# A hybrid decoder block on Trainium2: the norms of queries and keys, one tile of tokens at a time or four

## The chip, the cores and the metric

The kernel runs on one core of a Trainium2 chip. The metric is the device time of one execution in microseconds; lower is better. The engines are named as in the profile: PE (TensorE; PEld is its weight load), DVE (VectorE), ACT (ScalarE), POOL (GpSimd) and SP (SyncE, which here only issues DMAs).

## The reference

One decoder block over 1024 tokens of width 1024. Two token mixers run side by side: an attention of 8 heads of width 64 with a forgetting term, and a diagonal state-space model (SSM). Their gated sum goes through a projection, and a mixture of 32 experts follows. What matters here is the start of the attention:

```python
q = _rmsnorm(q.reshape(b, s, N_HEADS_ATTN, HEAD_DIM), q_norm_g[l])
k = _rmsnorm(k.reshape(b, s, N_HEADS_ATTN, HEAD_DIM), k_norm_g[l])
...
logits = jnp.einsum('bhqd,bhkd->bhqk', qb, kf) + cb[..., :, None] - cum[:, :, None, :]
```

where `_rmsnorm(x, g)` is `x * rsqrt(mean(x*x) + 1e-6) * g`, over the 64 values of one head. So for every token and head there is one factor for the query and one for the key.

## The kernel before

Tokens lie in tiles of 128 along the partitions, eight tiles in all. A matrix in 32-bit float is split into a high part and a remainder, so a product is three matmuls. The kernel goes through the SSM, the gates, the attention, the output projection with the router, and the experts, in this order; parts of neighbouring stages run into each other.

The attention takes two heads at a time, four pairs, and a pair in two halves of four tiles (512 tokens). Three generators do the work, and `run_all` interleaves their steps by a key, so that matmuls of one fill PE while others wait:

- `proj` (lines 783 to 813) computes queries, keys and values of one half. For each of its four tiles, 24 matmuls of 384 columns (lines 795 to 797) go into one PSUM bank; ACT copies queries and keys to the tile `qk` (800) and squares them in PSUM (801); DVE sums each group of 64 squares into four columns of `ss` (802) and takes the remainder of the values (807). Then comes the norm: scale and epsilon on DVE (808), a power with exponent -1/2 on POOL into `rstd` (809), and the multiplication of the 256 columns by the four factors, on POOL in place (811). `ss` and `rstd` have room for four tiles of tokens, four columns each. It is called eight times: for pair 0 half 0, pair 0 half 1, pair 1 half 0, and so on.
- `prep` (815 to 869) transposes the scaled keys (821) and queries (824) of a half, four tiles each, on PE; ACT and DVE split them into `KX`, `KY`, `QX`, `QY` (833 to 839); PE computes scores (852, with a mask at 855) only to find each row's maximum, by a reduction on DVE (857, 860). The maxima are transposed (862) and stored into rows of `QX` by two DMAs from POOL's queue (868, 869). Its transposes come some steps after the `proj` that it needs: in the meantime the next `proj` and an `attend` have put their own steps on PE.
- `attend` (871 to 941) computes scores again (901 to 904), takes the exponential twice on ACT (907, 909), forms the remainder `pL` on DVE (910), adds up the row sums on POOL (912, over `pe`, which has three buffers), and multiplies by the values (886, 887). At its end DVE splits the sums (`sh` on ACT, 923; `sl` on DVE, 925), PE spreads them (930) and DVE takes reciprocals (933) and scales.

During the last pair, `mixed_ssm` (its matmuls are at lines 700 to 702) fills PE, and line 671 splits its inputs on DVE.

The order within an engine's queue isn't the program's alone. A planner takes the instructions in program order as a priority, simulates when each could start, and gives an engine the first one that it believes ready. It also sets all semaphores. An engine then works through its queue in that order: an instruction whose input is late holds up all that stand behind it on that engine.

Of the kernel before, what the change touches and what calls it, by code (L numbers as in the profile page):

```python
# [16 lines left out]
ALU = mybir.AluOpType  # L17
AX = mybir.AxisListType

P = 128  # L20
# [5 lines left out]
DH = 64  # L26
G = 32
CG = 16
EPS = 1e-6
# [13 lines left out]
def hybrid_block(ctx: ExitStack, tc: tile.TileContext, t, out):  # L43

    nc = tc.nc
# [14 lines left out]
    def mmtile():  # L60
        return psA.tile([P, 512], F32, tag="A", name="psA_t")
# [4 lines left out]
    def f32(ap):  # L66
        return ap.bitcast(F32)
# [4 lines left out]
    def slot(name, shape=(S,), dt=F32, where=None):  # L72
        pl, n = where or (slab, SLOTS)
        return pl.tile([P] + list(shape), dt, tag="s4", name=name, bufs=n)
# [60 lines left out]
    mhalf = cp.tile([P, 4], F32, name="mhalf")  # L135
# [352 lines left out]
    with ExitStack() as st:  # L488
# [19 lines left out]
        for b in range(G // GB):  # L508
# [84 lines left out]
            for q4 in range(GB // 4):  # L593
# [7 lines left out]
                for r in range(4):  # L601
                    g = q4 * 4 + r
                    o = ps[:, r * P:(r + 1) * P]
# [179 lines left out]
    def proj(p_, half):  # L783

        qk = slot("qk", (4, 256))
        ss = ap_.tile([P, 4, 4], F32, name="ss", bufs=2)
        rstd = ap_.tile([P, 4, 4], F32, name="rstd", bufs=2)
        for r in range(4):
            i = half * 4 + r
            ps = mmtile()  # L790
            for k in range(KD):
                ah = hTh[k][:, i * P:(i + 1) * P]
                al = hTl[k][:, i * P:(i + 1) * P]
                wh, wl = p_.w[k]
                nc.tensor.matmul(ps[:, :384], ah, wh, start=(k == 0), stop=False)  # L795
                nc.tensor.matmul(ps[:, :384], ah, wl, start=False, stop=False)  # L796
                nc.tensor.matmul(ps[:, :384], al, wh, start=False, stop=(k == KD - 1))  # L797
                if k in (2, 5):
                    yield
            nc.scalar.copy(qk[:, r, :], ps[:, 0:256])  # L800
            nc.scalar.activation(ps[:, 0:256], ps[:, 0:256], AF.Square)
            nc.vector.tensor_reduce(ss[:, r, :], ps[:, 0:256].rearrange("p (a b) -> p a b", b=64),
                                    axis=AX.X, op=ALU.add)
            vs = ps[:, 256:384].rearrange("p (a b) -> p a b", b=64)
            vh = p_.V[:, i, :, 0, :]
            nc.scalar.copy(vh, vs)
            nc.vector.tensor_tensor(p_.V[:, i, :, 1, :], vs, f32(vh), ALU.subtract)
            nc.vector.tensor_scalar(ss[:, r, :], ss[:, r, :], 1.0 / DH, EPS, op0=ALU.mult, op1=ALU.add)
            nc.gpsimd.tensor_tensor(rstd[:, r, :], ss[:, r, :], mhalf, ALU.pow)
            q3 = qk[:, r, :].rearrange("p (a b) -> p a b", b=64)  # L810
            nc.gpsimd.tensor_tensor(q3, q3, rstd[:, r, :].unsqueeze(2).to_broadcast([P, 4, 64]), ALU.mult)
            yield
        p_.qk = qk

# [127 lines left out]

    cur = new_pair(0)
    run_all((proj(cur, 0), 12, 0, 1))
    run_all((proj(cur, 1), 12, 0, 1), (prep(cur, 0), 10, 0.3, 1))
    for pr in range(4):
        if pr < 3:
            nxt = new_pair(pr + 1)
            run_all((attend(cur, 0), 10, 0.1, 1), (proj(nxt, 0), 12, 0, 1), (prep(cur, 1), 10, 0.25, 1))
            if pr < 2:  # L950
                run_all((attend(cur, 1), 18, 0.1, 1), (proj(nxt, 1), 12, 0, 1), (prep(nxt, 0), 10, 0.3, 1))
            else:
                fill = mixed_ssm()
                run_all((attend(cur, 1), 18, 0.1, 1), (proj(nxt, 1), 12, 0, 0.9), (prep(nxt, 0), 10, 0.3, 1),
                        (itertools.islice(fill, 5), 5, 0.9, 1.1))
            cur = nxt
        else:
            wq_stack.close()
            slab2 = pool(ctx, "slab2")
            S2 = (slab2, SLOTS2)  # L960
            y3 = []
            ya, wgs = [], []

            def ready_a():

                for k in range(3):
                    ya.append(split_slot("a", yaT_d[k * P:(k + 1) * P, :], where=S2))
                    yield
                for mg in (0, 2):
                    wgs.append(mixed_weights(0, mg))  # L970
                    yield

            run_all((attend(cur, 0), 10, 0, 1), (itertools.islice(fill, 16), 16, 0, 1),
                    (prep(cur, 1), 10, 0.25, 1))
            run_all((attend(cur, 1, y3), 18, 0.1, 1), (fill, 32, 0, 1), (ready_a(), 5, 0.5, 0.95))
# [542 lines left out]
```

## Time and profile before

| | us |
|---|---|
| median of 3 runs | 1182.69 (1181.40 to 1185.41) |
| profiled execution | 1180.84 |
| its span | 1179.2 |
| PE busy | 1106.0 (94%) |
| DVE busy | 804.9 (68%) |
| ACT busy | 620.3 (53%) |
| POOL busy | 356.9 (30%) |

The mean granted clock of PE is 0.98. Line 808 has 32 instructions on DVE, line 809 has 32 and line 811 has 32 on POOL. They lie between 327.2 and 568.1 us of the span.

How to read the profile: the page's slices are 40 equal parts of the span, each digit the busy tenths of an engine. A row of the view by groups gives line, engine, operation, output<-input with shapes, count, then busy us, mean ns of one, and the idle time of the engine just before these instructions with what ended it. A row of the timeline gives start and duration in us, then the same names, and in brackets the idle time before it. A row of the waits gives the one that waited, the one that it waited for, us in total, count and longest.

### The profile page before, as it was taken

How to read it: one execution, taken by the hardware profiler on the slowest of the kernel's cores; microseconds unless marked ns; L12 is line 12 of the kernel's file. 1: busy time of each engine (PE TensorE's matmuls, PEld its weight loads, DVE VectorE, ACT ScalarE, POOL GpSimd, SP SyncE). 2: the span in 40 equal slices, each digit the busy share in tenths (PEclk: the TensorE clock that was granted, in tenths of full speed). 3: DMA queues.
4: the chain of work that ended last, by engine and by line, in shares of the span. 5: the costliest groups of instructions: out<-in, count | busy, mean ns of one | idle time of the engine just before them, and what ended most of it. 6: DMA issues, size and time to landing. Idle time of an engine off the chain costs nothing. (4 is left out here: it accounts for less than half of the span.)

```text
span 1179.2 us, 15928 instructions
## 1 busy us (share of the span) xinstructions
PE 1106.0 (94%) x5323; PEld 848.4 (72%) x5324; DVE 804.9 (68%) x1593; ACT 620.3 (53%) x1195; POOL 356.9 (30%) x399
## 2 busy tenths in 40 slices
PE   5999999999999999999899979997699999999995
PEld 4778878887897888788677868885466666666562
DVE  4986887964247899898986795529466666666660
ACT  5443233234246666658868452204376776666662
POOL 3110111013144565647443451102322222222211
PEclk9999999999999999999999999998799999999998
DMA  7625553321604030002523548554599999999992
GB/s 237 88 75 149 130 82 82 81 73 49 152 22 55 11 64 11 16 10 81 205 81 135 184 170 295 181 208 183 188 331 345 327 315 305 314 317 322 311 331 56
DMA packets 100918, 193.78 MB, mean 164 GB/s; under 512 B 26176, under 2 KB 55168, under 8 KB 100832
## 3 DMA queue, kind: packets, MB, share of 16 engines
q1 hardware_dynamic: 82176, 150.16, 41.5%
q0 software_dynamic: 14048, 34.17, 10.6%
q10 hardware_dynamic: 4608, 8.39, 1.9%
q8 instruction: 43, 0.70, 0.2%
q14 instruction: 43, 0.35, 0.1%
HBM read 164.30 MB, written 35.52 MB: 169 GB/s over the span
## 5 line engine op out<-in xcount | busy, mean ns | idle before, releaser
L1104 DVE TENSOR_TENSOR wel<-raw_e,weh 128x512 fp32r<-128x512 f32 x256 | 157.5, 686 | 116.9 <-ACT weh L1103 116.9
L1103 ACT CAST weh<-raw_e 128x512 fp32r<-128x512 f32 x256 | 137.2, 622 | 2.2 <-DVE wel L1104 0.8
L1379 PE MATMUL psA_t<-wd,hT 128*96 128x512 f32 x256 | 115.7, 594 | 3.0 <-DMA wd<-in_w_expert_down 2.2
L912 POOL TENSOR_TENSOR sm<-sm,pe 128x256 f32<-128x256 f32 (+2 forms) x80 | 96.1, 1202 | 70.3 <-ACT pe L909 62.0
L1354 PE MATMUL psA_t<-weh,xh 128*96 128x512 f32 x256 | 103.8, 406 | 0.2
L1355 PE MATMUL psA_t<-wel,xh 128*96 128x512 f32 x256 | 102.2, 399 | 0.0
L1356 PE MATMUL psA_t<-weh,xl 128*96 128x512 f32 x256 | 101.3, 396 | 0.0
L162 PE MATMUL psA_t<-hTl,wgh 128*128 128x512 f32 x256 | 100.7, 393 | 0.0
L161 PE MATMUL psA_t<-hTh,wgl 128*128 128x512 f32 x256 | 100.7, 393 | 0.0
L160 PE MATMUL psA_t<-hTh,wgh 128*128 128x512 f32 x256 | 100.5, 393 | 0.0
L795 PE MATMUL psA_t<-wqh,hTh 128*128 128x384 f32 x256 | 88.0, 344 | 0.0
L796 PE MATMUL psA_t<-wql,hTh 128*128 128x384 f32 x256 | 86.4, 338 | 0.0
L797 PE MATMUL psA_t<-wqh,hTl 128*128 128x384 f32 x256 | 86.3, 337 | 0.0
L1381 POOL DMA_INDIRECT out_rows<-R,ix x32 | 46.0, 1438 | 127.3 <-ACT hT L1370 116.1
L1380 ACT ACTIVATE R<-psA_t,wts 96x512 f32<-96x512 f32 x64 | 43.7, 682 | 75.8 <-PE psA_t L1379 73.7
L1379 PEld LDWEIGHTS psA_t<-wd,hT 128*96 128x96 f32 x256 | 40.0, 167 | 55.0 <-issue 48.9
L1330 POOL DMA_INDIRECT XG<-xn_d,ix x32 | 35.8, 1119 | 139.0 <-PE psB_t L1341 133.1
L907 ACT ACTIVATE pH<-psB_t 128x512 fp32r<-128x512 f32 (+1 forms) x96 | 49.1, 511 | 36.4 <-PE psB_t L904 36.2
L910 DVE TENSOR_TENSOR pL<-pe,pH 128x256 fp32r<-128x256 f32 (+2 forms) x80 | 62.5, 793 | 6.5 <-ACT pe L909 5.7
L164 ACT COPY ge<-psA_t 128x512 f32<-128x512 f32 x32 | 18.7, 584 | 86.6 <-PE psA_t L162 81.8
L857 DVE TENSOR_REDUCE mx<-psB_t 128x1 f32<-128x512 f32 (+2 forms) x96 | 51.2, 551 | 6.2 <-PE psB_t L855 2.7
L1163 PE MATMUL psA_t<-woh,mxh 128*128 128x512 f32 x128 | 54.3, 424 | 1.2 <-DVE gt L988 1.2
(425 smaller groups left out, 2828.7 us busy)
## 6 DMA issues: line engine op xcount, KB each, us to landing
raw_e<-in_w_expert_gate SPq DMA_DIRECT2D x64, 512.0 KB
raw_e<-in_w_expert_up SPq DMA_DIRECT2D x64, 512.0 KB
wd<-in_w_expert_down SPq DMA_DIRECT2D x64, 512.0 KB
gate_d<-ge ACTq DMA_DIRECT2D x32, 256.0 KB
gt<-gate_d SPq DMA_DIRECT2D x16, 512.0 KB
raw_g<-in_w_in SPq DMA_DIRECT2D x12, 512.0 KB
raw_q<-in_w_in SPq DMA_DIRECT2D x48, 128.0 KB
x<-in_x SPq DMA_DIRECT2D x8, 512.0 KB
```

Of the source, the lines that this page charges most:

```text
L160: nc.tensor.matmul(ps, wh, hTh[k][:, ns], start=(k == 0), stop=False)
L161: nc.tensor.matmul(ps, wl, hTh[k][:, ns], start=False, stop=False)
L162: nc.tensor.matmul(ps, wh, hTl[k][:, ns], start=False, stop=(k == KD - 1))
L795: nc.tensor.matmul(ps[:, :384], ah, wh, start=(k == 0), stop=False)
L796: nc.tensor.matmul(ps[:, :384], ah, wl, start=False, stop=False)
L912: nc.gpsimd.tensor_tensor(sm[:, o0:], sm[:, o0:], pe[:, :n], ALU.add)
L1103: nc.scalar.copy(wh[d_], src)
L1104: nc.vector.tensor_tensor(wl[d_], src, f32(wh[d_]), ALU.subtract)
L1354: nc.tensor.matmul(ps, xh[:, k, :], wh[:, k % 2, :], start=(k == 0), stop=False)
L1355: nc.tensor.matmul(ps, xh[:, k, :], wl[:, k % 2, :], start=False, stop=False)
L1356: last = nc.tensor.matmul(ps, xl[:, k, :], wh[:, k % 2, :], start=False, stop=(k == KD - 1))
L1379: pe = nc.tensor.matmul(po, hT[:, j, :], wd[j][:, ns], start=(j == 0), stop=(j == 1))
```

## The change

In `proj`, the scale with epsilon and the power are taken out of the work of the single tile. Once the sums of the fourth tile are there, one DVE instruction scales all 16 columns of `ss`, one POOL instruction raises them to -1/2 (its exponent is one column of `mhalf` read 16 times), and four POOL instructions multiply the four tiles of `qk`, one after the other. Everything else stays: the sums, the copies, the values' remainder, the places of the generators' steps and the tiles' buffers.

```diff
             nc.vector.tensor_tensor(p_.V[:, i, :, 1, :], vs, f32(vh), ALU.subtract)
-            nc.vector.tensor_scalar(ss[:, r, :], ss[:, r, :], 1.0 / DH, EPS, op0=ALU.mult, op1=ALU.add)
-            nc.gpsimd.tensor_tensor(rstd[:, r, :], ss[:, r, :], mhalf, ALU.pow)
-            q3 = qk[:, r, :].rearrange("p (a b) -> p a b", b=64)
-            nc.gpsimd.tensor_tensor(q3, q3, rstd[:, r, :].unsqueeze(2).to_broadcast([P, 4, 64]), ALU.mult)
+            if r == 3:
+                nc.vector.tensor_scalar(ss, ss, 1.0 / DH, EPS, op0=ALU.mult, op1=ALU.add)
+                nc.gpsimd.tensor_tensor(rstd.rearrange("p r a -> p (r a)"), ss.rearrange("p r a -> p (r a)"),
+                                        mhalf[:, 0:1].to_broadcast([P, 16]), ALU.pow)
+                for o in range(4):
+                    q3 = qk[:, o, :].rearrange("p (a b) -> p a b", b=64)
+                    nc.gpsimd.tensor_tensor(q3, q3, rstd[:, o, :].unsqueeze(2).to_broadcast([P, 4, 64]), ALU.mult)
             yield
```

## The prediction

> **What bounds the kernel now.** I read the page's slices first, then the stretch in which the changed lines run, then what TensorE waits for there.
>
> ```profile
> PE   5999999999999999999899979997699999999995
> DVE  4986887964247899898986795529466666666660
> POOL 3110111013144565647443451102322222222211
> ```
>
> ```profile
> core 0: us, PE busy (x) PEld busy (x) DVE busy (x) ACT busy (x) POOL busy (x), PEclk, DMA share, GB/s
> 326.00:568.00 242.00, 232.54 (x1308) 199.43 (x1306) 200.00 (x376) 154.50 (x352) 144.03 (x158) 1.00 0.17 41
> ```
>
> TensorE (PE) is nearly full in almost every slice. The second fence is the view by stretches, from the first norm of queries and keys to the last: of 242.00 us PE is busy 232.54, VectorE (DVE) 200.00 and GpSimd (POOL) 144.03, at a granted clock of 1.00. PE is the bound; what another engine saves counts only where PE waits for it. Those waits, in the same stretch:
>
> ```profile
> PE acc L887 <- DVE pL L910: 3.6, 7, 0.9
> PE psB_t L852 <- ACT KY L839: 1.1, 3, 0.5
> PE psB_t L852 <- DVE mx L857: 1.1, 1, 1.1
> PE acc L886 <- ACT pH L907: 0.7, 2, 0.4
> PE psB_t L862 <- DVE mx L860: 0.7, 1, 0.7
> PE psB_t L862 <- DVE mx L857: 0.6, 1, 0.6
> PE psB_t L821 <- POOL rstd L809: 0.4, 1, 0.4
> ```
>
> The columns are total us, count, longest. Waits for DVE, or for ScalarE (ACT) behind it, come to 3.6+1.1+1.1+0.7+0.7+0.6 = 7.8 us; waits for the norm's own GpSimd work to 0.4.
>
> **What goes.** There are eight calls of the projection (four pairs of heads, two halves), each with four tiles of tokens; I number the calls 0 to 7. Line 808 (scale and epsilon) and line 809 (power) fall from 32 to 8 instructions each; the scalings of line 811 stay 32.
>
> ```profile
> L808 DVE TENSOR_SCALAR ss<-ss 128x4 f32<-128x4 f32 x32 | 8.8, 274 | 0.4
> L925 DVE TENSOR_TENSOR sl<-sm,sh 128x512 fp32r<-128x512 f32 x16 | 11.3, 706 | 3.7 <-ACT sh L923 3.5
> ```
>
> ```profile
> L1206 POOL TENSOR_TENSOR rstd<-rstd,mhalf x8: 558/559/576, 721.3 to 814.5; 128x1 f32<-128x1 f32 x8
> ```
>
> ```profile
> L809 POOL TENSOR_TENSOR rstd<-ss,mhalf x32: 1006/1032/2073, 327.9 to 565.0; 128x4 f32<-128x4 f32 x32
> ```
>
> ```profile
> L811 POOL TENSOR_TENSOR qk<-qk,rstd x32: 603/613/943, 329.0 to 567.1; 128x256 f32<-128x256 f32 x32
> ```
>
> (Minimum, median and maximum in ns.) DVE loses 24 x 0.274 = 6.6 us of its 200. No row has a power over sixteen columns. One column takes 0.559 us, four take 1.032, so a column adds (1.032-0.559)/3 = 0.158 and sixteen would take 0.559+15x0.158 = 2.93 us. Bounds: 1.03 if the count of columns hardly mattered, 4 x 1.032 = 4.13 if the work were simply four times the old one. The two rows lie on a slope, so I take 2.93. GpSimd then spends 8 x 2.93 = 23.4 us on powers against 32 x 1.032 = 33.0: 9.6 us less (between 25 less and nothing less), on an engine with 98 us idle in the stretch. By itself that is worth nothing on PE's path.
>
> **What DVE's relief is worth.** All 6.6 us could count only if PE waited for each; the bound is the 7.8 us above, the floor 0. One place can be followed:
>
> ```profile
> 398.30 0.85 DVE L808 TENSOR_SCALAR ss<-ss 128x4 f32<-128x4 f32 x1
> 399.06 1.94 DVE L910 TENSOR_TENSOR pL<-pe,pH 128x512 fp32r<-128x512 f32 x3
> 400.93 0.74 DVE L836 SCALAR_TENSOR_TENSOR KY<-psB_t,gk,KX 64x512 fp32r<-64x512 f32 x1
> ```
>
> ```profile
> 401.70 0.68 ACT L839 ACTIVATE KY<-psB_t,gk 64x512 fp32r<-64x512 f32 x1 [0.60 <-DVE KY L836]
> ```
>
> Here the small scaling of the first tile of call 3 takes 0.85 us, and behind it on DVE stand three differences and the split of the keys, for which ACT waits; PE's three waits for that (1.1 us) are in the list. Removing the scaling should take most of the 1.1 away. Of the 3.6 us at line 887 I take a quarter, 0.9, since 6.6 us out of 200 thins DVE's queue little. Relief: 2 us.
>
> **What comes later.** All four scalings now follow the last tile's power. From the start of that power to the last scaled tile it was 1.03+0.08+0.61 = 1.72 us (0.08 is the gap between the two). It becomes 2.93+4x0.613 = 5.38 us, 3.7 more; bounds 1.03+2.45 = 3.5 and 4.13+2.45 = 6.6. Behind it wait the four transposes of keys at line 821 (the queries' at 824 need nothing more). They run in PE's own order, so if they come late everything behind them on PE does. The last tile's power:
>
> ```profile
> 337.55 1.01 POOL L809 TENSOR_TENSOR rstd<-ss,mhalf 128x4 f32<-128x4 f32 x1 [2.46 <-DVE ss L808]
> 358.40 1.04 POOL L809 TENSOR_TENSOR rstd<-ss,mhalf 128x4 f32<-128x4 f32 x1
> 359.41 0.59 POOL L869 DMA_DIRECT2D QX<-ml  x1
> 390.59 1.03 POOL L809 TENSOR_TENSOR rstd<-ss,mhalf 128x4 f32<-128x4 f32 x1 [5.07 <-DVE mx L860]
> 392.26 0.57 POOL L868 DMA_DIRECT2D QX<-mh  x1
> 394.76 1.28 POOL L912 TENSOR_TENSOR sm<-sm,pe 128x512 f32<-128x512 f32 x1 [1.39 <-ACT pe L909]
> 428.05 1.03 POOL L809 TENSOR_TENSOR rstd<-ss,mhalf 128x4 f32<-128x4 f32 x1 [2.97 <-DVE ss L808]
> 564.98 2.07 POOL L809 TENSOR_TENSOR rstd<-ss,mhalf 128x4 f32<-128x4 f32 x1
> ```
>
> and the weight loads of the transposes that use it:
>
> ```profile
> 341.52 0.54 PEld L821 LDWEIGHTS psB_t<-ident,qk 128*128 128x128 f32 x4
> 342.46 0.19 PEld L795 LDWEIGHTS psA_t<-wqh,hTh 128*128 128x128 f32 x1
> 361.44 0.51 PEld L821 LDWEIGHTS psB_t<-ident,qk 128*128 128x128 f32 x4
> 398.27 0.59 PEld L821 LDWEIGHTS psB_t<-ident,qk 128*128 128x128 f32 x4
> 432.84 0.51 PEld L821 LDWEIGHTS psB_t<-ident,qk 128*128 128x128 f32 x4
> 567.45 0.31 PEld L821 LDWEIGHTS psB_t<-ident,qk 128*128 128x128 f32 x3 [0.59 <-POOL rstd L809]
> 568.13 0.14 PEld L821 LDWEIGHTS psB_t<-ident,qk 128*128 128x128 f32 x1 [0.37 <-POOL qk L811]
> 568.13 0.25 PEld L930 LDWEIGHTS psA_t<-sl,sel 128*128 128x128 f32 x1
> ```
>
> The fourth load of a group of four begins about 0.4 us after the first. Call 0: scaled at 337.55+5.38 = 342.9, wanted at 341.9: 1.0 late. Call 1: 363.8, or 364.4 if the DMA of line 869 stays between power and scaling, wanted at 361.8: 2.0 to 2.6 late. Call 2: 396.0 against 398.7, 2.7 spare; calls 4 and 6 repeat it. Call 3: 433.4 against 433.2, 0.2 late; call 5 repeats it. Call 7: 564.98+5.38 = 570.4, or 571.4 with the 1.04 us that its power lost (below), against 568.13, where PE waits already: 2.2 to 3.3 late. Sum, with PE's order as it is: 1.0+2.3+0.4+2.7 = 6.4 us. With a power of 1.03 only call 7 is late, by 0.3 to 1.4 us; with 4.13 it is 6.4+5x1.2 = 12.4.
>
> That order need not stay. The two last rows show it: the four products of line 930 come from one loop, yet a transpose of call 7 runs ahead of the loop's next one. The planner that orders each engine's queue moves ready work forward. At the three late places there is other work to put ahead: after call 0 the next tile's projection (the row at 342.46), after call 1 the same, after call 7 the mixer's products. But what the planner believes a sixteen-column power costs no row shows, and in call 7 it was early by the two waits of 0.59 and 0.37. I count half of the 6.4 us: 3.2.
>
> On GpSimd the burst of 5.4 us stands ahead of the stores of row maxima (lines 868 and 869) and of the sums of line 912. After call 2 the sum at 394.76 would start some 2 us late; the first-tile norm of the next call, 1.03+0.61 us, that stood behind those sums is gone, so the lag closes in that run. Three `pe` buffers cover it; without that cover ACT's exponentials, and PE behind them, would lose the 2 us in each of calls 2, 4 and 6.
>
> **The port, row first.**
>
> ```profile
> 428.72 0.69 DVE L925 TENSOR_TENSOR sl<-sm,sh 128x512 fp32r<-128x512 f32 x1
> ```
>
> ```profile
> 564.95 1.21 DVE L671 TENSOR_TENSOR yls<-yrs,yhs 128x1024 fp32r<-128x1024 f32 x1
> ```
>
> The difference at 428.72 began while call 3's power ran (428.05 to 429.08) and took 0.69 us, against the 0.706 mean of its line; held until the power's end, it would have taken 0.36 more. A power did not hold it up. The other way round, call 7's power began with the long difference of line 671 and took 2.07 us instead of 1.03. The Trainium skill, "SBUF — State Buffer", section "SBUF: two separate sides", says that GpSimd and a VectorE operation with two SBUF inputs share one port pair, that whoever starts first holds it for the whole instruction, and that the other blocks fully. The second case agrees with this, the first does not.
>
> **Sum.** 3.2 late transposes less 2 of relief: +1.2 us. The profiled execution took 1180.84 us, its span 1179.2 with 1.6 around it, so 1180.84+1.2 = 1182.0. The median shown is 1182.69, 1.85 above the profiled one; I forecast against the median: 1182.69+1.2 = 1183.9, 1184.
>
> **Rivals.**
> 1. The planner leaves the transposes where they stand. The late scalings of calls 0, 1 and 7 stop PE for 6.4 us (up to 12.4), relief gives back 1 to 2: +5, 1187.7. For it: PE already waits at call 7, and no row shows that the planner knows the price of a power. Against: ready work is there. It decides from about 5.5 us of stall, where less 2 it passes 3.5. Chance 0.25.
> 2. The planner hides the transposes fully, and a DVE queue with 24 fewer entries releases most of the 7.8 us: -5, 1177.7. For it: DVE is busy 200 of 242 us, and its small scalings are stretched by GpSimd's sums, as in the 0.85 us row. Against: the waits at line 857 and 860 are for a reduction that itself follows PE. Chance 0.2.
> 3. A power of 2.93 us holds DVE for all its length: 2.93-0.69 = 2.2 us for each of the two-input differences beside it in calls 3, 5 and 7, where `sl` feeds PE's line 930: +6.6 on top of the forecast, 1190.5. This is what the quoted rule of the "SBUF — State Buffer" page of the Trainium skill would give. The row at 428.72 speaks against it. Chance 0.05.
>
> **How the numbers follow.** The forecast has 0.5. A measurement of this kernel tells about 0.3%, 3.5 us, from no change, so faster means under 1179.2 and slower over 1186.2; the forecast's own range is these two. Rival 2 is faster (0.2), rivals 1 and 3 slower (0.3). The range takes in rival 1 and 2 at their centres, with the lesser part of their tails: 1177.5 to 1189.5.
>
> **What would show it.** Line 809's successor should last near 2.9 us, eight times; if 1.1, the late transposes vanish and rival 2 gains. Weight loads of line 821 should show waits for the scalings in calls 0, 1 and 7, or stand later in PE's order with projection products before them. PE's waits for KY should shrink. Waits for GpSimd at line 821 above 5 us in all would prove rival 1; a difference of line 925 or 910 that lasts 2 us or more beside a power, rival 3. The forecast fails if the whole plan after the stretch falls out differently, since then the sum says nothing.

## The result, and the profile after

The changed kernel takes 1198.18 us (median of 6 runs, 1192.81 to 1199.22), the kernel before 1183.08 us beside it (6 runs, 1181.40 to 1185.41). The ratio is 1.0118, with a 95% interval of 1.0095 to 1.0141: about 15 us slower, where I had forecast 1184 and given at most 1189.5. The profiled execution took 1198.93 us, its span 1197.2 against 1179.2; this pair of traces lies 18.0 us apart, more than the medians. One execution of the kernel one_three below took 1740.17 us at a granted clock of 0.59, and no ratio here counts it.

The diff adds three lines ahead of `prep`, so line 809 of the changed kernel is the old 808, 810 the old 809, and every line from 811 on has a number three higher. The kernels of the experiments keep the numbers of the kernel before.

First the changed instructions, from the views of single lines of the changed kernel (minimum, median and maximum in ns, first and last start):

```profile
L809 DVE TENSOR_SCALAR ss<-ss x8: 156/166/175, 337.7 to 578.6; 128x16 f32<-128x16 f32 x8
```

```profile
L810 POOL TENSOR_TENSOR rstd<-ss,mhalf x8: 2922/2927/3963, 338.0 to 580.0; 128x16 f32<-128x16 f32 x8
```

Eight of each, and the power of sixteen columns takes 2.93 us, as worked out. GpSimd and VectorE both have less to do. Now what TensorE waits for, between 326 and 590 us of the changed kernel (total us, count, longest):

```profile
PE psB_t L824 <- POOL qk L814: 4.4, 7, 2.6
PE psB_t L855 <- ACT pe L912: 4.2, 2, 2.1
PE psB_t L865 <- DVE mx L860: 3.6, 2, 2.2
PE psB_t L904 <- ACT pe L912: 2.4, 1, 2.4
PE acc L890 <- DVE pL L913: 1.2, 3, 0.8
```

The last row is the wait that I hoped to shrink, and it did, from 3.6 us to 1.2. The four above it are new or grown. The first is the late transposes. The second and the fourth are three stalls of 2.1, 2.1 and 2.4 us after calls 2, 4 and 6 that I had declared covered; the third is the row maxima of calls 3 and 5. Before, nothing on the prediction's list was longer than 1.1 us. In the view by stretches of the changed kernel the granted clock is the third number from the end of a row:

```profile
345.00:370.00 25.00, 23.69 (x129) 20.61 (x128) 17.32 (x31) 15.29 (x32) 8.84 (x10) 0.93 0.45 59
370.00:400.00 30.00, 29.32 (x167) 25.75 (x166) 24.96 (x49) 18.32 (x44) 12.76 (x14) 1.00 0.03 6
400.00:430.00 30.00, 27.60 (x150) 23.13 (x149) 25.94 (x37) 20.06 (x44) 20.52 (x18) 0.94 0.12 21
430.00:445.00 15.00, 12.83 (x67) 11.47 (x66) 11.42 (x23) 7.98 (x19) 7.63 (x9) 0.89 0.39 88
445.00:480.00 35.00, 34.74 (x199) 30.19 (x198) 31.68 (x58) 21.06 (x49) 18.50 (x20) 1.00 0.04 12
480.00:510.00 30.00, 25.69 (x133) 21.21 (x132) 23.84 (x38) 19.98 (x44) 16.45 (x14) 0.94 0.08 20
```

Before, the clock was 1.00 throughout this stage, up to 590 us; now it falls in each stretch in which TensorE waits long. Cut finer, it falls to 0.50 for a piece of 3.41 us behind the waits of call 1, after calls 2, 3, 4 and 6, and for 6.83 us in call 7. The piece after call 2 in the changed kernel, then a piece that the kernel before has too, just behind the stage:

```profile
410.70:414.10 3.40, 3.31 (x10) 2.80 (x11) 1.46 (x5) 2.44 (x7) 0.91 (x1) 0.50 0.02 5
```

```profile
590.07:593.48 3.41, 3.41 (x12) 2.74 (x11) 2.74 (x6) 2.11 (x4) 1.06 (x3) 0.50 0.47 157
```

**Where the time went.** I lined up the start of every matmul of the two traces, line by line in order; TensorE's order is nearly the same. The lag of the changed kernel grows from 0.4 us ahead of the first late transpose to 19.4 us at 592 us of its span; behind that the kernel before loses some of its lead in its own slow piece, and at the end the lag is 18.0 (1197.2 - 1179.2). The steps up to 592 us:

| what | where | us |
|---|---|---|
| transposes wait for the scalings | calls 0, 1, 7: 0.9, 2.1, 3.1 | 6.1 |
| next key block late | after calls 2, 4, 6: 1.9, 1.8, 2.5 | 6.2 |
| row maxima late | calls 3, 5: 1.5, 1.4 | 2.9 |
| matmuls at half rate | six places, after calls 1, 2, 3, 4, 6 and in 7: 0.8, 1.1, 1.5, 1.4, 1.7, 1.3 | 7.8 |
| what is left over: waits of before that are gone | the rest | -4.0 |
| sum | | 19.0 |

**Late transposes.** From the timeline of TensorE in the changed kernel (start, duration; in brackets the idle time before):

```profile
342.80 0.33 PE L824 MATMUL psB_t<-ident,qk 128*128 128x128 f32 x1 [0.24 <-POOL qk L814]
343.37 0.33 PE L824 MATMUL psB_t<-ident,qk 128*128 128x128 f32 x1 [0.24 <-POOL qk L814]
```

```profile
363.94 0.33 PE L824 MATMUL psB_t<-ident,qk 128*128 128x128 f32 x1 [0.60 <-POOL qk L814]
364.51 0.33 PE L824 MATMUL psB_t<-ident,qk 128*128 128x128 f32 x1 [0.24 <-POOL qk L814]
```

and of GpSimd in call 7:

```profile
580.00 3.96 POOL L810 TENSOR_TENSOR rstd<-ss,mhalf 128x16 f32<-128x16 f32 x1
584.04 2.32 POOL L814 TENSOR_TENSOR qk<-qk,rstd 128x256 f32<-128x256 f32 x4
```

The first two transposes of call 0 run on time, since two tiles are scaled by then; each later one waits for its own. In call 1 all four wait, 0.60 us at most. In call 7 the power took 3.96 us, a microsecond over its median, as its short predecessor did at the same place.

**The stalls after calls 2, 4 and 6**, in call 2. GpSimd in the changed kernel:

```profile
393.20 2.92 POOL L810 TENSOR_TENSOR rstd<-ss,mhalf 128x16 f32<-128x16 f32 x1 [5.72 <-DVE mx L863]
396.20 2.91 POOL L814 TENSOR_TENSOR qk<-qk,rstd 128x256 f32<-128x256 f32 x4
399.06 0.57 POOL L871 DMA_DIRECT2D QX<-mh  x1
399.63 0.54 POOL L872 DMA_DIRECT2D QX<-ml  x1
400.19 4.70 POOL L915 TENSOR_TENSOR sm<-sm,pe 128x512 f32<-128x512 f32 x3
```

VectorE, ScalarE and TensorE in the changed kernel, one view each:

```profile
400.47 4.97 DVE L913 TENSOR_TENSOR pL<-pe,pH 128x512 fp32r<-128x512 f32 x3
405.36 0.73 DVE L839 SCALAR_TENSOR_TENSOR KY<-psB_t,gk,KX 64x512 fp32r<-64x512 f32 x1
```

```profile
406.13 0.68 ACT L842 ACTIVATE KY<-psB_t,gk 64x512 fp32r<-64x512 f32 x1 [2.22 <-DVE KY L839]
```

```profile
404.13 0.33 PE L796 MATMUL psA_t<-wql,hTh 128*128 128x384 f32 x1
404.30 0.33 PE L797 MATMUL psA_t<-wqh,hTl 128*128 128x384 f32 x1
...
409.48 0.39 PE L855 MATMUL psB_t<-KX,QX 66*128 66x256 f32 x1 [2.12 <-ACT pe L912]
...
411.01 0.52 PE L795 MATMUL psA_t<-wqh,hTh 128*128 128x384 f32 x1
411.33 0.52 PE L796 MATMUL psA_t<-wql,hTh 128*128 128x384 f32 x1
```

And GpSimd at the same place of the kernel before:

```profile
396.43 2.69 POOL L912 TENSOR_TENSOR sm<-sm,pe 128x512 f32<-128x512 f32 x2 [0.39 <-ACT pe L909]
399.06 0.56 POOL L941 DMA_DIRECT2D yaT_d<-yu  x1
399.64 1.05 POOL L809 TENSOR_TENSOR rstd<-ss,mhalf 128x4 f32<-128x4 f32 x1
400.76 0.72 POOL L811 TENSOR_TENSOR qk<-qk,rstd 128x256 f32<-128x256 f32 x1
401.44 2.57 POOL L912 TENSOR_TENSOR sm<-sm,pe 128x512 f32<-128x512 f32 x2
```

Before, VectorE's three differences (the row at 399.06 in the prediction, 1.94 us) ran while GpSimd issued a DMA and worked on the first tile's norm: 0.65 us each. Now they run beside three row sums in a row and take 4.97 us, 1.66 each. The split of the keys stands behind them on VectorE, ScalarE waits 2.22 us for it and TensorE 2.12 for ScalarE. The row names the exponential, which ScalarE did behind that split. So the delay passes through VectorE's queue, not through the three buffers of `pe`, and in the kernel before it was the first tile's norm that kept the sums away from the differences.

Which of the two waits depends on which starts first. In the row at 400.47 each of the three differences began while a sum ran. Where a difference begins first, it keeps its 0.69 us and the sum grows from 1.28 to 1.73, as here in the changed kernel (VectorE, then GpSimd):

```profile
421.28 0.69 DVE L913 TENSOR_TENSOR pL<-pe,pH 128x512 fp32r<-128x512 f32 x1
```

```profile
421.39 1.73 POOL L915 TENSOR_TENSOR sm<-sm,pe 128x512 f32<-128x512 f32 x1 [0.24 <-ACT pe L912]
```

After the stall, the two matmuls at 411.01 and 411.33 start 0.32 us apart, where those at 404.13 and 404.30, ahead of it, are 0.17 apart; the pace is back by 414.

**The row maxima in calls 3 and 5.** VectorE in the changed kernel, TensorE behind it, and VectorE before:

```profile
432.14 0.96 DVE L765 TENSOR_TENSOR wql<-raw_q,wqh 128x768 fp32r<-128x768 f32 x1 [2.01 <-ACT wqh L764]
```

```profile
434.09 0.27 PE L865 MATMUL psB_t<-ident,mx 128*4 128x128 f32 x1 [2.17 <-DVE mx L860]
```

```profile
425.80 0.96 DVE L765 TENSOR_TENSOR wql<-raw_q,wqh 128x768 fp32r<-128x768 f32 x1 [0.44 <-ACT wqh L764]
```

VectorE stands 2.01 us (0.44 before) ahead of the remainder of a reloaded weight, with the reduction queued behind it.

### The profile page after: what moved, and what is told of

It is laid out like the page before. It is cut to its first block, busy times and chain, and to the rows that moved or that the text cites. A ratio compares the mean times of both kernels' runs of the same rounds, so it can differ in the third digit from the quotient of the medians.

```text
span 1197.2 us, 15893 instructions
## 1 busy us (share of the span) xinstructions
PE 1113.8 (93%) x5323; PEld 856.5 (72%) x5324; DVE 809.8 (68%) x1569; ACT 621.4 (52%) x1195; POOL 349.8 (29%) x375
## 3 DMA queue, kind: packets, MB, share of 16 engines
q0 software_dynamic: 14048, 34.17, 10.4%
## 5 line engine op out<-in xcount | busy, mean ns | idle before, releaser
L915 POOL TENSOR_TENSOR sm<-sm,pe 128x256 f32<-128x256 f32 (+2 forms) x80 | 99.9, 1249 | 97.8 <-ACT pe L912 95.5
L913 DVE TENSOR_TENSOR pL<-pe,pH 128x256 fp32r<-128x256 f32 (+2 forms) x80 | 68.0, 861 | 7.5 <-ACT pe L912 6.4
```

Source lines behind the costliest of these rows:

```text
L915: nc.gpsimd.tensor_tensor(sm[:, o0:], sm[:, o0:], pe[:, :n], ALU.add)
```

## The experiments

Four theories were put against each other. A: the burst of norm work on GpSimd at the end of a call holds up what stands behind it there. B: what costs is that the power is now one long instruction. C: the planner ordered the work differently, and the loss is chance. D, formed after the first runs, also called the pause theory: the short power of the first tile is a pause in which GpSimd leaves VectorE the port to SBUF that the two share by the rule that the prediction quotes; without it, row sums and differences collide.

Beside the medians I read the stretch from the first to the last matmul of line 797, from first and last start in its row, which holds all eight calls and nothing of the later stages; with the same code, the rest of the span differs by some us between these profiles. A stretch comes from one execution each. For the kernel before and the changed one:

```profile
L797 PE MATMUL psA_t<-wqh,hTl x256: 333/335/422, 319.6 to 559.0; 128*128 128x384 f32 x128
```

```profile
L797 PE MATMUL psA_t<-wqh,hTl x256: 332/336/527, 320.1 to 575.2; 128*128 128x384 f32 x128
```

That is 239.4 and 255.1 us. All runs (ratio to the kernel before on the same chip; the last column is the mean of VectorE's 24 differences of 512 columns over `pe`, in ns):

| kernel | median, us | ratio [95%] | stretch over before, us | difference |
|---|---|---|---|---|
| before | | 1 | 0 | 875 |
| changed | 1198.18 | 1.0118 [1.0095, 1.0141] | +15.7 | 1208 |
| defer | 1193.14 | 1.0090 [1.0066, 1.0113] | +12.2 | 1146 |
| pairs | 1192.90 | 1.0082 [1.0053, 1.0110] | +14.2 | 1187 |
| three_one | 1198.96 | 1.0153 [1.0128, 1.0178] | +14.7 | 1177 |
| after_nopow | 1198.29 | 1.0154 [1.0109, 1.0198] | +16.4 | 1204 |
| three_one_spare | 1192.31 | 1.0092 [1.0061, 1.0124] | +4.4 | 809 |
| after_spare | 1197.77 | 1.0132 [1.0105, 1.0160] | +14.0 | 1021 |
| before_nopow | 1190.81 | 1.0075 [1.0054, 1.0097] | +9.1 | 1122 |
| one_two_one | 1184.13 | 1.0013 [0.9995, 1.0031] | +1.8 | 810 |
| one_three | 1187.22 | 1.0023 [0.9997, 1.0048] | +5.2 | 849 |
| before_nosums | 1357.77 | 1.1450 [1.1401, 1.1498] | -5.2 | 718 |
| after_nosums | 1365.74 | 1.1521 [1.1476, 1.1566] | -0.1 | 727 |

**defer**: the four norms come after the fourth tile, each with its own instructions.

```diff
+            for o in (range(4) if r == 3 else ()):
-            nc.vector.tensor_scalar(ss[:, r, :], ss[:, r, :], 1.0 / DH, EPS, op0=ALU.mult, op1=ALU.add)
-            nc.gpsimd.tensor_tensor(rstd[:, r, :], ss[:, r, :], mhalf, ALU.pow)
+                nc.vector.tensor_scalar(ss[:, o, :], ss[:, o, :], 1.0 / DH, EPS, op0=ALU.mult, op1=ALU.add)
+                nc.gpsimd.tensor_tensor(rstd[:, o, :], ss[:, o, :], mhalf, ALU.pow)
...
```

> All four norms wait for the fourth tile, but each stays as it was: four small scales, four powers of four columns, four scalings. The whole reference is computed. Theory A (a burst of about 6 us on GpSimd at the end of each projection call is what costs: late transposes, row sums pushed onto VectorE's differences, a slower TensorE clock after each stall): the burst is 4 x 1.64 = 6.6 us against 5.8 in the changed kernel, though its first scaled tiles come earlier, so +12 to +20 us on the kernel before. Theory B (a single power of 2.9 us that cannot be divided is what costs): no power is over 1.03 us, so within +4 us of the kernel before. Theory C (the planner's other order of queues costs): anything, without a relation to the burst.

Measured 1193.14 us, slower than before by 0.9% (11.0 us, just under theory A's 12 to 20 and far from theory B's 4), with not one instruction joined or removed. So the joining is not needed for most of the loss; moving the norms is enough. Its row sums run from 400.07 without the first tile's norm between them, and TensorE stalls at the next key block as in the changed kernel.

**pairs** and **three_one**: tiles joined two and two, and three and one. A table by `r` gives the first tile of each joined norm, which ends at tile `r`: `((), (0,), (), (2,))` and `((), (), (0,), (3,))`.

```diff
+            for o0 in TABLE[r]: nc.vector.tensor_scalar(ss[:, o0:r + 1], ss[:, o0:r + 1], 1.0 / DH, EPS, op0=ALU.mult, op1=ALU.add)
+            for o0 in TABLE[r]: nc.gpsimd.tensor_tensor(rstd[:, o0:r + 1].rearrange("p r a -> p (r a)"), ss[:, o0:r + 1].rearrange("p r a -> p (r a)"), mhalf[:, 0:1].to_broadcast([P, 4 * (r + 1 - o0)]), ALU.pow)
+            for o in [o for o0 in TABLE[r] for o in range(o0, r + 1)]:
...
```

> Norms for two tiles at a time, after the second and after the fourth tile; the whole reference is computed. The power has eight columns, about 1.7 us, two scalings follow, so a burst of 2.9 us against 1.7 in the kernel before and 5.8 in the changed one. Theory A: the last tile is some 1.2 us later than before, so only call 7 and perhaps call 1 stop TensorE; +1 to +5 us on the kernel before. Theory B: a power of 1.7 us; +3 to +6. Theory C: as far from the kernel before as the changed one, +10 or more, since its queues change as well.

> Norms for three tiles at once after the third, and for the fourth alone as before; the whole reference is computed. Power of twelve columns about 2.3 us and three scalings, a burst of 4.1 us, but at the third tile; the end of a call is as in the kernel before. Theory A with the end of the call as the place: no late transposes and no pushed row sums behind the fourth tile, so within 3 us of the kernel before, perhaps 1 to 2 us faster by the VectorE instructions saved. Theory A with the burst as such, wherever it stands: +5 to +10. Theory B: a power of 2.3 us; +7 to +11. Theory C: +10 or more.

Both are as slow or nearly so, and theory A had forecast them too fast (10.8 us over before for pairs where it said 1 to 5, 16.9 for three_one where it said within 3, or 5 to 10; theory C's 10 or more fits both), though three_one leaves the last tile's norm as it was, so that no transpose comes late behind a burst. The timelines of three_one show why. GpSimd, then VectorE, of three_one:

```profile
399.13 0.58 POOL L941 DMA_DIRECT2D yaT_d<-yu  x1
399.73 1.30 POOL L912 TENSOR_TENSOR sm<-sm,pe 128x512 f32<-128x512 f32 x1
```

```profile
398.38 4.63 DVE L910 TENSOR_TENSOR pL<-pe,pH 128x512 fp32r<-128x512 f32 x3
402.94 0.74 DVE L836 SCALAR_TENSOR_TENSOR KY<-psB_t,gk,KX 64x512 fp32r<-64x512 f32 x1
```

Up to 399.7 all runs as before. Then, in the place of the first tile's power, the next row sum moves up, and the three differences take 4.63 us in place of 1.94. The split of the keys begins at 402.94, two microseconds after its 400.93 of before. Here no burst pushes the sums, so theory A alone is not enough: the sums are not pushed but pulled into the gap.

**after_nopow**: the changed kernel without the power; the tiles are scaled by the scaled sums.

```diff
-                nc.vector.tensor_scalar(ss, ss, 1.0 / DH, EPS, op0=ALU.mult, op1=ALU.add)
-                nc.gpsimd.tensor_tensor(rstd.rearrange("p r a -> p (r a)"), ss.rearrange("p r a -> p (r a)"),
-                                        mhalf[:, 0:1].to_broadcast([P, 16]), ALU.pow)
+                nc.vector.tensor_scalar(ss, ss, 4e-4, EPS, op0=ALU.mult, op1=ALU.add)
```

> The changed kernel without the power: the four scalings at the end multiply by the scaled sums themselves, so the norms of queries and keys are not those of the reference; everything else stays. The burst is 4 x 0.6 = 2.4 us. Theory A: little over the old 1.7 us, so within +3 us of the kernel before. Theory B: no power at all, so within 2 us, or faster. Theory C: the order is nearly that of the changed kernel, +10 or more. If it stays at +10, neither the length of the power nor that of the burst is the cause, but four scalings in a row.

1198.29 us, as slow as the changed kernel, with no power in it. Theory B falls. After call 2 its burst is short enough to leave the sums in time (396.19 us, against 396.43 before), but the next sum stands at 399.40, in the place of the first tile's norm, and the three differences take 4.63 us, as in three_one. What remained was that a power does something useful in the kernel before.

**three_one_spare** and **after_spare**: a scale and a power over the first tile's sums, into a tile that nobody reads, are put back at the place where the kernel before has them.

```diff
+            if r == 0:
+                nc.vector.tensor_scalar(spare[:, r, :], ss[:, r, :], 1.0 / DH, EPS, op0=ALU.mult, op1=ALU.add)
+                nc.gpsimd.tensor_tensor(spare[:, r, :], spare[:, r, :], mhalf, ALU.pow)
```

> The kernel with norms for three tiles and then one, to which the first tile's own small scale and power are added again, into a spare tile that nobody reads; the result is the whole reference. Theory D (a power does not hold the port to SBUF that GpSimd's sums and VectorE's differences share, so the first tile's power after calls 2, 4 and 6 is a pause in which three differences pass; without it the sums run on and block each one): work that nobody needs makes the kernel faster, the three waits for the keys' split go back to those of the kernel before (about 1.9 us less each) with the slow clock behind them (1.1 to 1.5 us each), so from +17 to about +8 us on the kernel before. Theory A (the burst of three norms): +17 or a little more. Theory C (another plan): no rule, but not less than +12.

> The changed kernel with the same spare scale and power for the first tile; the whole reference is computed. Theory D alone: about -9 us on the changed kernel, so +6 on the kernel before. Theory D with A (in the changed kernel the burst of 5.8 us at the end of calls 2, 4 and 6 itself pushes the sums onto the differences, and the spare power stands behind those sums): nothing is won, +13 to +17.

Useless work makes three_one faster: 1192.31 against 1198.96, and the stretch 10.3 us shorter. GpSimd, then VectorE, of three_one_spare:

```profile
400.56 1.59 POOL L807 TENSOR_TENSOR spare<-spare,mhalf 128x4 f32<-128x4 f32 x1
402.14 2.56 POOL L912 TENSOR_TENSOR sm<-sm,pe 128x512 f32<-128x512 f32 x2
```

```profile
399.97 1.88 DVE L910 TENSOR_TENSOR pL<-pe,pH 128x512 fp32r<-128x512 f32 x3
```

The three differences are back at 0.63 us each; the power beside them took 1.59 us instead of 1.03. So the power gives way to the differences, and a sum that has begun does not. The median gained less than the stretch: it is still 10.0 us over before, where theory D alone said 8 and theory C at least 12. The trace shows part of the rest behind the stretch: at 567.4 us TensorE stalls for 2.37, with four row sums in a row on GpSimd (5.11 us from 568.09, behind the joined norm of call 7) and on VectorE a scale of 1.56 us ahead of the difference that TensorE wants; behind it the clock is 0.50 from 570.0 to 576.9. Its lag on the kernel before grows there from 4.2 to 8.3 us. In the changed kernel the same spare work hardly helps (1197.77): there the sums are pushed behind the burst and meet the differences (4.07 us) before the spare power's turn at 406.00. So there are two ways into the same collision: in the changed kernel the burst alone is enough, in three_one and after_nopow the missing pause alone.

**before_nopow**: the kernel before without its 32 powers.

```diff
-            nc.vector.tensor_scalar(ss[:, r, :], ss[:, r, :], 1.0 / DH, EPS, op0=ALU.mult, op1=ALU.add)
-            nc.gpsimd.tensor_tensor(rstd[:, r, :], ss[:, r, :], mhalf, ALU.pow)
+            nc.vector.tensor_scalar(ss[:, r, :], ss[:, r, :], 4e-4, EPS, op0=ALU.mult, op1=ALU.add)
...
```

> The kernel before without its 32 powers: each tile is scaled by its scaled sums, so the norms are not those of the reference; everything else stays, tile by tile. Theory D: 33 us of GpSimd work less make the kernel slower, since the pauses go: +6 to +12 us. Theories A and B: no burst and no power, so within 2 us of the kernel before, or faster.

33 us of GpSimd's work are gone, nothing is joined or delayed, and the kernel is slower by 8.5 us (1190.81 against 1182.28), as theory D forecast and A and B did not. The groups of VectorE's differences, between 320 and 590 us, say why: before, changed, before_nopow, in this order (busy us, mean ns):

```profile
L910 DVE TENSOR_TENSOR pL<-pe,pH 128x512 fp32r<-128x512 f32 x24 | 20.6, 875 | 0.7 <-ACT pe L909 0.4
```

```profile
L913 DVE TENSOR_TENSOR pL<-pe,pH 128x512 fp32r<-128x512 f32 x24 | 28.6, 1208 | 1.9 <-ACT pe L912 1.3
```

```profile
L910 DVE TENSOR_TENSOR pL<-pe,pH 128x512 fp32r<-128x512 f32 x24 | 26.6, 1122 | 1.6 <-ACT pe L909 1.3
```

**one_two_one** and **one_three**: the first tile's norm alone, as before; then tiles 1 and 2 joined and the last alone, `((0,), (), (1,), (3,))`, or all three others joined behind the last, `((0,), (), (), (1,))`. The edit is the table of pairs.

> Norms for the first tile alone, the next two together after the third, the last alone; the whole reference is computed. Theory D: the first tile's power stays in its place and the end of a call is as before, so -1 to +4 us on the kernel before. Theory C: the queues change as much as in the other groupings, +10.

> Tile 0 has its norm alone, with its own short power; tiles 1, 2 and 3 get theirs together after the last tile, with a power of 12 columns (about 2.3 us by 1.03 us for 4 and 2.92 us for 16) and three scalings of 0.61 us. Pause theory: the short power of tile 0 still stands ahead of the row sums after calls 2, 4 and 6, so the three differences there keep their 0.65 us each and the stalls at the weights of the next key block do not appear; what stays is the late transposes, by less than in the changed kernel, since 4.1 us stand behind the last tile's sums and not 5.4. Time 1184 to 1190. Rival, that joining norms behind the last tile costs whatever is left at tile 0: within 3 us of the changed kernel, 1195 to 1200.

one_two_one, which differs from three_one in the place of the first tile's norm (its joined norm is of two tiles and not of three), can't be told from before (0.9995 to 1.0031) and is 15 us faster than three_one. No slow matmuls appear in the stretch, and its differences average 810 ns. This also speaks against theory C: the order was disturbed here too, and by joining, without loss. one_three adds the late transposes of a power of twelve columns and two pieces at half clock (from 431.1 and 574.4 us). It is 5 us slower at the median, as forecast, but its interval includes 1, and the profiled execution was the slowest of its fast ones (1190.64), so a loss is likely and not shown.

**before_nosums** and **after_nosums**: both kernels without the row sums. Since the factors differ, other tokens go to the experts, with one block more in both kernels, and TensorE waits there for a transfer that the other kernels don't need; so their times can be compared with each other alone, and the stretches with all.

```diff
-                if kt:
-                    nc.gpsimd.tensor_tensor(sm[:, o0:], sm[:, o0:], pe[:, :n], ALU.add)
...
-            nc.scalar.copy(sh, sm)
+            nc.scalar.activation(sh, sm, AF.Copy, bias=1.0)
-            nc.vector.tensor_tensor(sl, sm, f32(sh), ALU.subtract)
+            nc.vector.tensor_tensor(sl, sm, f32(sh), ALU.add)
```

> The kernel before without the additions that GpSimd makes for the row sums (line 912); the factor is taken from the first block's exponentials plus one, so the output is not the reference's. This is the base for the next run. Pause theory: the additions cost little in the kernel before, where pauses lie between them: time 1174 to 1183. Rival, that they hold VectorE up in the kernel before as well: below 1170.

> The changed kernel without the additions for the row sums (line 912), left out as in the run before this one. Pause theory: nothing that holds the port is left behind the long power, so the stalls after calls 2, 4 and 6 vanish with the slow clock behind them; the late transposes of calls 0, 1 and 7 stay. Its time stands 4 to 9 us over that of the kernel before without the additions. Rival, that the burst itself costs what was measured, with or without the additions: 13 to 18 us over it.

The wait in the experts, of before_nosums, and the stretch of each:

```profile
PE psB_t L1341 <- DMA xgd<-xn_d,dx: 132.1, 1, 132.1
```

```profile
L797 PE MATMUL psA_t<-wqh,hTl x256: 333/336/422, 320.7 to 554.9; 128*128 128x384 f32 x128
```

```profile
L797 PE MATMUL psA_t<-wqh,hTl x256: 333/335/522, 320.5 to 559.8; 128*128 128x384 f32 x128
```

The base missed its expected time, 1174 to 1183 us, by that wait and the added block. The comparison of the two stands (8.0 us between the medians, 4 to 9 expected), and more sharply in the stretch, 234.2 and 239.3 us: without the sums the change costs 5.1 us there, with them 15.7. Two thirds of the loss need the row sums. That agrees with the table of steps, where the late key blocks and the half rate behind them take 6.2+1.1+1.4+1.7 = 10.4 us. What is left is mainly the late transposes, for which TensorE waits there too (5.4 us at line 821 in after_nosums). The sums cost the kernel before 5.2 us as well: even there the differences average 875 ns, and 718 without sums.

## Why the prediction was wrong

**Right: the length of the power.** 2.93 us estimated, 2.927 measured at the median; the line through one and four columns held at sixteen.

**Right in place, and I halved it: the late transposes.** 1.0, 2.3 and 2.7 us for calls 0, 1 and 7; measured 0.9, 2.1 and 3.1. The 0.4 us of calls 3 and 5 did not come, since TensorE itself was late there. The planner did not move other work ahead: the half that I took off for it was wrong, and rival 1 was right in this. The transposes' weight loads waited 7.4 us for GpSimd, above the 5 that I had set as its sign. (One bound of mine was off: with a power of 1.03 us call 1 would have been up to 0.6 us late too, not call 7 alone.)

**Not shown: the relief.** I took 2 us, half from the keys' split and half from line 887. Waits worth some 4.0 us disappeared, but otherwise than I said: line 887's lost 2.4 us, while the waits behind the keys' split became the three stalls. TensorE also came late to many of them, and one_two_one, which saves eight scalings, waits 4.6 us at line 887; no run shows that VectorE's saved instructions are the reason.

**Failed: "Three `pe` buffers cover it".** This step cost most: a term that I put at nothing, against 6.2 us of stalls and 4.2 of the half rate behind them. I saw that the row sums after call 2 would start some 2 us late, named calls 2, 4 and 6 and priced the loss without cover at 2 us each: 6 us. That 6.2 was measured is luck, since my 2 us was the lag of the sums and not the stretch of the differences (from 1.94 to 4.97 us). I looked for cover only among the buffers of what the sums read. But sums and differences also hold each other up, and the sums' new place was beside the three differences. I had the row that shows a small scaling stretched to 0.85 us beside the sums, and the row of three differences at 0.65 us each beside a power; what I did not ask is how long these differences are beside a sum. The trace before holds the answer, at the sum of 394.76 that I had listed:

```profile
394.98 1.61 DVE L910 TENSOR_TENSOR pL<-pe,pH 128x512 fp32r<-128x512 f32 x1
```

The sentence that the first-tile norm is gone, "so the lag closes", had it backwards: that norm was the gap.

**The port rule.** The prediction set the rule of the Trainium skill, "SBUF — State Buffer", section "SBUF: two separate sides", against the row of a power that held nobody up, and gave the blocking power a chance of 0.05. That power indeed blocks nothing (0.63 us a difference beside it in three_one_spare). But the same rule, that whoever starts first keeps the pair for a whole instruction and the other blocks, is what the row sums do: 1.66 us a difference beside sums of 1.3 to 1.6, and 0.69 where the difference began first. I tested the rule on the operation that the change makes longer, and not on those that it moves.

**Missing: the clock.** I had no term for 7.8 us of matmuls at half pace. In the stretch that I read the kernel before shows none, but 22 us behind it there is one, after a stall of 1.35 us at 588.0 us, and I had not looked there. So rival 1, nearest in mechanism with 1187.7, was short by the 6.2 of the sums, the 7.8 of the clock and the 2.9 of the row maxima, against which 4.0 us of waits and not 1 to 2 came back.

**"By itself worth nothing"**, said of GpSimd's saved powers, was too kind: taking them all out costs 8.5 us.

**Open.** The 2.9 us of the row maxima I read off one pair of traces (a weight's remainder waits longer on VectorE, with the reduction behind it); no run isolates it, and the wait is also there in one_three (3.5 us), where the differences are no longer than before, and not in defer (0.6, as before). Part of the loss of three_one_spare behind the stretch is unexplained. No version here beats the kernel before.

## What to carry to other kernels

When an instruction goes from an engine whose work holds up another's, as GpSimd's sums and VectorE's differences do here, look at what moves up into its place and what the other engine does at that moment: idle time of the one engine, or an operation that gives way, like the power here, can be the window in which the other runs. Ask for each moved operation how long its neighbour's instructions take beside it, from rows where the two overlap, and not only whether its buffers last. Where a change makes TensorE stall for a microsecond or more, reckon with slow matmuls behind the stall too: in the changed kernel they added 0.8 to 1.7 us a time.

## What I had not expected of the hardware

**A power and a sum, both on GpSimd, treat VectorE differently.** Three differences of 512 columns take 1.88 us beside a power of four columns, which itself grows from 1.03 to 1.59; beside row sums they take 4.63 to 4.97 us.

**Half pace after a stall.** In the changed kernel, behind every stall of 2.1 to 2.6 us and behind the four short waits of call 1, the granted clock is 0.50 for 3.41 or 6.83 us, and the matmuls of 384 columns start every 0.32 us in place of 0.17, which costs 0.8 to 1.7 us each time; a stall of 1.4 us left nothing of the kind. The length of the stall alone doesn't decide: 1.35 us was enough in the kernel before (the row at 590.07), and 2.05 us at 428.5 in three_one was not. The Trainium skill, "TensorE: Matmul & The Clock Gate", section "Part 1: The HAM clock gate (the "warmup" mystery)", describes two states, full and half clock, and gives an idle window of about 3.4 us before the clock drops. The half rate agrees with the trace: 384 columns at the page's 1.2 GHz make an estimate of 0.32 us, and 0.32 was measured. The window does not: here shorter stalls were enough.
